# Small matmuls of a chunked scan: heads placed on partitions by the parity of their pair, not of their chunk

## The chip, the core and the metric

The kernel runs on one core of a Trainium2 chip. TensorE (PE in the profile) multiplies through an array of 128 rows by 128 columns; VectorE (DVE), ScalarE (ACT) and GpSimd (POOL) do the elementwise work; SyncE (SP) issues the DMAs here. The metric is device time in microseconds (us), the median of several executions. A row of the profile such as "32*32 32x64" says which part of the array a matmul uses (32 rows, 32 columns) and what it writes (32 partitions by 64 elements).

## What is computed

The reference is one block with an RWKV-7 branch, a short convolution, a cross attention and an MLP, followed by a second block with windowed attention and spatial gating. The change touches the RWKV-7 branch alone. With 8 heads of 64 channels and 512 positions, each head carries a 64x64 state S through the positions:

```
for t in positions:
    S = S * decay[t] + v[t] k[t]^T + (S a[t]) b[t]^T
    y[t] = S r[t]
y = group_norm(y) * ln_x_w + ln_x_b + bonus
out = (y * g) @ w_proj_a
```

The kernel does this in 8 chunks of 64 positions. Within a chunk the recurrence is a triangular system; its two 32x32 diagonal blocks are inverted ahead of time, and the chunk itself is matmuls.

## The kernel before

Everything is one function, `fused_kernel`, written as dataflow on tiles; a scheduler turns it into one fixed order for each engine, higher in the program meaning earlier where operands and buffers allow it. Large projections are done as three matmuls of 128x512 for each weight tile (L182 to L184, weights split in a high and a low part by L152 on ACT and L153 on DVE), and the scheduler fills PE with those of later stages while the scan waits for something.

The eight heads are four pairs j = 0 to 3. `KB` and `AR` hold keys and receptances with the two heads of a pair on partitions 0 to 63 and 64 to 127; `VU` holds, for each chunk and head, 64 rows of v and 64 rows of u (the solution of the triangular system), together 128 partitions. In the kernel before, the chunk's parity c = n % 2 says which half is which: in an even chunk all heads have v on partitions 0 to 63 and u on 64 to 127, in an odd chunk the reverse. The output of a matmul stands on the partitions that answer to the array's columns, so all small matmuls of one chunk use the same half of the columns.

`scan_front(tb)` makes the products of keys and receptances for two chunks (`gram`, L386, masked by L390 on DVE) and inverts the diagonal blocks (`inverse`): the blocks go through DRAM by DMA (L400, L407), 31 steps on DVE (L413, L415) follow, and the inverse comes back by DMA as `ZT` (L419, L425). The loop calls `scan_front(tb + 1)` before the two chunks of tb. `chunk(n, ...)` then is, with its lines:

- L437, L439: the pair's keys are transposed (PE) and copied (ACT) to `KBt`.
- L443: 8 matmuls, one for each head, K = 128 rows, 64 columns, 64 elements each, into the bank `pg`; L447: 4 matmuls of 128 elements add the state's part to it.
- L455, L458, L460: the first 32 rows are copied (ACT), multiplied by the inverse block in 8 matmuls of 32 rows by 32 columns, and copied to `VU` (DVE).
- L462, L464, L467, L469: the second 32 rows: 8 matmuls of 32 by 32 for the correction, copy, 8 matmuls with the inverse block, copy.
- L474, L478, L481: the new state: 4 matmuls of 128x128 with one product for a whole pair, scaled by the decay `PC` (which holds zeros where the heads of a pair must not mix) and added to the old state that POOL has scaled (`spc`, L451). L481 ends the chain that the next chunk's L447 waits for.
- L488, L491: the outputs, 4 matmuls of 128 elements and 8 of 64, into one bank `py` for two chunks. `post(tb)` normalises them.

All of these are plain fp32 matmuls: PE runs each as two passes, each with its own weight load, and the profile counts passes. Eight matmuls stand in a row as x16. Transposes are one pass.

## Time and profile before

| | |
|---|---|
| median of 3 executions | 1340.09 us (1336.71 to 1343.22) |
| the profiled execution: its time, its span | 1343.95 us, 1342.1 us |
| PE busy | 1302.3 us, 97% of the span |
| DVE, ACT, POOL busy | 814.8 us, 520.5 us, 174.4 us |
| DMA queue q1, share of 16 engines | 34.0% |
| granted clock of TensorE, mean | 0.989 |

PE is busy nearly everywhere, but the profile counts a pipelined matmul as busy from its start to its modelled end, so that the time of one row is read from start to start. The granted clock is 1.00 where TensorE runs at 2.4 GHz and 0.5 at 1.2 GHz. The scan's chunks stand in four stretches: the first products at 142 to 152 us, then chunk pairs at 204 to 235, 272 to 305 and 342 to 395 us (two pairs). Between them PE works on large projections while DVE does the 31 steps of the next inverse.

### The profile page before, as it was taken

What the parts mean: (1) busy time and instruction counts of PE and PEld (TensorE: products, weight loads), DVE (VectorE), ACT (ScalarE), POOL (GpSimd) and SP (SyncE); (2) the same over time, 40 slices, a digit from 0 to 9 for tenths busy, and PEclk for the clock granted to TensorE, in tenths of its full rate; (3) what the DMA queues carried; (4) which work ended last, traced back from release to release, by engine and by line L of the source; (5) the groups of instructions that cost most, each with busy time, mean ns of one, the idle gap of its engine ahead of it and who ended that gap; (6) DMA issues with size and microseconds to landing.
All of it is one profiled execution on the core that took longest, in us unless ns stands there. A gap on an engine that the chain in (4) does not pass through costs nothing.

```text
span 1342.1 us, 18317 instructions
## 1 busy us (share of the span) xinstructions
PE 1302.3 (97%) x6626; PEld 1069.7 (80%) x6626; DVE 814.8 (61%) x1631; ACT 520.5 (39%) x940; POOL 174.4 (13%) x184
## 2 busy tenths in 40 slices
PE   3999999999999999999999999999999999999997
PEld 2777888888879888888888888888878777788886
DVE  5677484848466755566854645535676656663455
ACT  4444232322335443454532423323344465333342
POOL 5113002010120010002012020020232000100003
PEclk9999999989999999999999999999999999999999
DMA  4222331314314532143643634332234223233331
GB/s 143 87 79 67 101 104 43 110 44 123 90 63 150 173 110 94 64 149 94 186 152 110 194 112 145 128 96 87 94 126 142 79 63 125 87 97 101 94 118 63
DMA packets 85210, 143.95 MB, mean 107 GB/s; under 512 B 21472, under 2 KB 21600, under 8 KB 85120
## 3 DMA queue, kind: packets, MB, share of 16 engines
q1 hardware_dynamic: 85120, 142.78, 34.0%
q8 instruction: 52, 0.85, 0.3%
q14 instruction: 38, 0.31, 0.1%
HBM read 136.19 MB, written 5.24 MB: 105 GB/s over the span
## 4 chain that ended last, share of the span: by engine, by line
PE 94%; DVE 3%; POOL 1%; DMA 1%; issue 0%; ACT 0%; SPq 0%; DVEq 0%; ACTq 0%; POOLq 0%
PE mm L182 26%; PE mm L183 26%; PE mm L184 25%; PE mm L627 1%; PE mm L628 1%; PE mm L629 1%; PE sc L386 1%; PE ch L943 1%; PE ch L978 1%; PE ch L458 1%; PE ch L467 1%; DMA x<-in_xT 1%; PE sc L974 1%; PE ch L462 1%; PE ch L491 1%; PE ch L474 1%
## 5 line engine op out<-in xcount | busy, mean ns | idle before, releaser
L152 ACT CAST whi<-wraw 128x512 fp32r<-128x512 f32 x406 | 251.7, 621 | 551.7 <-PE mm L183 475.7
L153 DVE TENSOR_TENSOR wlo<-wraw,whi 128x512 fp32r<-128x512 f32 x406 | 298.4, 736 | 228.1 <-PE mm L184 118.6
L182 PE MATMUL mm<-h,whi 128*128 128x512 f32 x328 | 132.5, 404 | 1.0 <-DVE k L237 1.0
L183 PE MATMUL mm<-h,whi 128*128 128x512 f32 x328 | 131.4, 401 | 0.0
L184 PE MATMUL mm<-h,wlo 128*128 128x512 f32 x328 | 131.1, 400 | 0.0
L182 PE MATMUL mm<-x2g,whi 128*128 128x512 f32 x256 | 100.2, 391 | 0.0
L184 PE MATMUL mm<-x2g,wlo 128*128 128x512 f32 x256 | 99.7, 389 | 0.0
L183 PE MATMUL mm<-x2g,whi 128*128 128x512 f32 x256 | 99.6, 389 | 0.0
L182 PE MATMUL mm<-ff,whi 128*128 128x512 f32 x256 | 99.6, 389 | 0.0
L183 PE MATMUL mm<-ff,whi 128*128 128x512 f32 x256 | 99.6, 389 | 0.0
L184 PE MATMUL mm<-ff,wlo 128*128 128x512 f32 x256 | 99.6, 389 | 0.0
L182 PEld LDWEIGHTS mm<-h,whi 128*128 128x128 f32 x328 | 62.8, 192 | 16.2 <-DVE k L237 2.6
L183 PEld LDWEIGHTS mm<-h,whi 128*128 128x128 f32 x328 | 62.7, 191 | 13.1 <-issue 0.4
L184 PEld LDWEIGHTS mm<-h,wlo 128*128 128x128 f32 x328 | 62.5, 190 | 13.3 <-issue 0.5
L852 POOL TENSOR_TENSOR X<-X,d 128x512 f32<-128x512 f32 x24 | 39.3, 1637 | 220.8 <-DVE d L850 220.8
L658 POOL TENSOR_TENSOR gt<-gt,nsq 128x512 f32<-128x512 f32 x21 | 27.7, 1320 | 291.5 <-ACT nsq L657 284.0
L183 PE MATMUL mm<-h2a,whi 128*128 128x512 f32 x152 | 59.7, 393 | 0.4 <-DVE h2a L875 0.4
L184 PE MATMUL mm<-h2a,wlo 128*128 128x512 f32 x152 | 59.8, 393 | 0.0
L182 PE MATMUL mm<-h2a,whi 128*128 128x512 f32 x152 | 59.7, 395 | 0.0
L182 PE MATMUL mm<-h2b,whi 128*128 128x512 f32 x152 | 59.7, 392 | 0.0
L184 PE MATMUL mm<-h2b,wlo 128*128 128x512 f32 x152 | 59.5, 393 | 0.0
L183 PE MATMUL mm<-h2b,whi 128*128 128x512 f32 x152 | 59.5, 392 | 0.0
(465 smaller groups left out, 2700.7 us busy)
## 6 DMA issues: line engine op xcount, KB each, us to landing
wraw<-in_w_in SPq DMA_DIRECT2D x162, 256.0 KB, 2.6
wraw<-in_w_up SPq DMA_DIRECT2D x64, 256.0 KB, 2.6
wraw<-in_w_down SPq DMA_DIRECT2D x64, 256.0 KB, 2.8
adaraw<-in_w_ada SPq DMA_DIRECT2D x24, 512.0 KB, 3.7
wraw<-in_w_proj_b SPq DMA_DIRECT2D x16, 256.0 KB, 2.7
wraw<-in_w_k SPq DMA_DIRECT2D x16, 256.0 KB, 2.6
wraw<-in_w_proj_a SPq DMA_DIRECT2D x16, 256.0 KB, 2.7
wraw<-in_w_v SPq DMA_DIRECT2D x16, 256.0 KB, 2.7
```

Of the source, the lines that this page charges most:

```text
L152: S.copy(hi, src)
L153: eng.tensor_tensor(lo, src, hi.bitcast(F32), op=ALU.subtract)
L182: PE.matmul(acc, lhsT=wh, rhs=xh, start=start and k == 0, stop=False)
L183: PE.matmul(acc, lhsT=wh, rhs=xl, start=False, stop=False)
L184: PE.matmul(acc, lhsT=wl, rhs=xh, start=False, stop=stop and k == n - 1)
L386: PE.matmul(pq[hd % 2][:, j * 128:(j + 1) * 128], lhsT=KB[p0:p0 + 64, j, n * 128:(n + 1) * 128], rhs=AR[p0:p0 + 64, j, n].rearrange("p q c ...
L458: PE.matmul(pu[ub:ub + 32, hs], lhsT=ZT[ub:ub + 32, c, hd, :], rhs=gsb[ub:ub + 32, hs], start=True, stop=True)
L462: PE.matmul(pg[ub + 32:ub + 64, hd * 64:(hd + 1) * 64], lhsT=gr[ub:ub + 32, hd, 32:64], rhs=VU[ub:ub + 32, tb, c, hd, :], start=False, sto ...
L467: PE.matmul(pu[ub + 32:ub + 64, hs], lhsT=ZT[ub + 32:ub + 64, c, hd, :], rhs=gsb[ub + 32:ub + 64, hs], start=True, stop=True)
L474: PE.matmul(pst[:, j * 128:(j + 1) * 128], lhsT=KBt[:, 2 * j:2 * j + 2, :].rearrange("p h f -> p (h f)"), rhs=VU[:, tb, c, 2 * j:2 * j + 2 ...
L658: G.tensor_tensor(self.acc, self.acc, sq, op=ALU.add)
L852: G.tensor_tensor(X[:, j], X[:, j], d, op=ALU.add)
```

## The change

The parity of the pair, j % 2, takes the place of the chunk's parity: pairs 0 and 2 have v on partitions 0 to 63 and u on 64 to 127, in every chunk, pairs 1 and 3 the reverse. The loops over heads run in the order `order8`, in which the pair's parity `jp` changes fastest, so that one matmul writes to the upper half of the partitions and the next to the lower. What follows from it:

- All banks of a chunk hold 256 elements on 128 partitions in place of 512 on 64: `pg`, `pu`, `py`. The copies change with them (one of 128x256 for `gh`; the two halves of `VU` by DVE and ACT, 32x256 each; `y` by one copy for each chunk, from its own bank).
- The 32-row matmuls of the two parities use different rows and different columns of the array, and write the same bank.
- The state's product (L474) becomes 8 matmuls of 64 columns and 64 elements, alternating halves too. The state update is one DVE operation of 256 columns (`s1`) and two of 64x256, and POOL scales `s1` for the chunk after.
- `KB`, `bon`, `g` and the weights `w_lora_g`, `ln_x` are laid out to match: `g` by four activations of 64x256 in place of one of 128x512, for each of four blocks; `KB` by one DVE operation less; `bon` by one more.
- The DMAs of the inverse (to `md` and back to `ZT`) are 8 in place of 4, of half the heads each.
- `gram` puts pairs in another column order, its matmuls are the same.

```
...
-        kb = KB[:, j].rearrange("p (m x) -> p m x", x=256)
-        V.scalar_tensor_tensor(kb[:, :, 64:192], halves(ta), 1.0, halves(m1), op0=ALU.add, op1=ALU.mult)
-        V.tensor_tensor(kb[:, :, 0:64], halves(f)[:, :, 0:64], halves(ip)[:, :, 0:64], op=ALU.mult)
-        V.tensor_tensor(kb[:, :, 192:256], halves(f)[:, :, 64:128], halves(ip)[:, :, 64:128], op=ALU.mult)
+        kb = KB[:, j].rearrange("p (n x) -> p n x", x=128)
+        ub, vb = 64 * (1 - j % 2), 64 * (j % 2)
+        V.scalar_tensor_tensor(kb[:, :, ub:ub + 64], chunks(ta), 1.0, chunks(m1), op0=ALU.add, op1=ALU.mult)
+        V.tensor_tensor(kb[:, :, vb:vb + 64], chunks(f), chunks(ip), op=ALU.mult)
...
-        S.activation(g, p, AF.Copy, scale=0.5)
+        for c in range(2):
+            for jp in range(2):
+                S.activation(g[64 * jp:64 * jp + 64, 256 * c:256 * c + 256],
+                             p[64 * c:64 * c + 64, 256 * jp:256 * jp + 256], AF.Copy, scale=0.5)
...
+    order8 = [(hp, jh, jp) for hp in range(2) for jh in range(2) for jp in range(2)]
...
+        blocks = [(i, d, jp, ((i * 2 + d) * 2 + jp) * 4, 64 * (1 - jp) + 32 * d)
+                  for i in range(2) for d in range(2) for jp in range(2)]
+        for i, d, jp, q0, r0 in blocks:
+            nc.sync.dma_start(md[q0:q0 + 4].rearrange("h j i -> j h i"),
+                              grams[i][r0:r0 + 32, 4 * jp:4 * jp + 4, 32 * d:32 * d + 32])
...
-        for hd in range(8):
-            PE.matmul(pg[ub:ub + 64, hd * 64:(hd + 1) * 64], lhsT=gr[:, hd, 0:64],
-                      rhs=VU[:, tb, c, hd, :], start=hd == 0, stop=n == 0 and hd == 7)
+        for hp, jh, jp in order8:
+            ub, b = 64 * (1 - jp), 2 * jh + hp
+            PE.matmul(pg[ub:ub + 64, b * 64:(b + 1) * 64], lhsT=gr[:, 4 * jp + b, 0:64],
+                      rhs=VU[:, n, 4 * jp + b, :], start=b == 0, stop=n == 0 and b == 3)
...
+        for d in range(2):
+            S.copy(gh[:, d], pg[:, 0:256])
+            for hp, jh, jp in order8:
+                r0, b = 64 * (1 - jp) + 32 * d, 2 * jh + hp
+                hs = slice(b * 64, (b + 1) * 64)
+                PE.matmul(pu[r0:r0 + 32, hs], lhsT=ZT[r0:r0 + 32, c, b, :], rhs=gh[r0:r0 + 32, d, hs],
+                          start=True, stop=True)
+            for jp in range(2):
+                r0 = 64 * (1 - jp) + 32 * d
+                (V.tensor_copy, S.copy)[jp](VU[r0:r0 + 32, n, 4 * jp:4 * jp + 4, :],
+                                            pu[r0:r0 + 32, 0:256].rearrange("p (h v) -> p h v", v=64))
...
-                PE.matmul(pst[:, j * 128:(j + 1) * 128], lhsT=KBt[:, 2 * j:2 * j + 2, :].rearrange("p h f -> p (h f)"),
-                          rhs=VU[:, tb, c, 2 * j:2 * j + 2, :].rearrange("p h v -> p (h v)"),
-                          start=j == 0, stop=j == 3)
+                g0 = 4 * (j % 2) + 2 * (j // 2)
+                for hp in range(2):
+                    PE.matmul(pst[64 * hp:64 * hp + 64, j * 64:(j + 1) * 64], lhsT=KBt[:, 2 * j + hp, :],
+                              rhs=VU[:, n, g0 + hp, :], start=j == 0, stop=j == 3)
...
+                V.tensor_tensor(s1, ps_, comp[0], op=ALU.add)
...
+            for hp in range(2):
+                rows = slice(64 * hp, 64 * hp + 64)
+                V.tensor_tensor(sn[rows, :, 64 * hp:64 * hp + 64], s1[rows], pc[rows], op=ALU.mult)
...
```

The scheduler puts the scan's groups among the large products in another order; behind the scan, PE's order is the same as before. Two places show what moved. The first is PE in chunk 1, between the two products with the inverse block. Rows name line, operation, output and inputs; `gsb` and `gh` are the copies of `pg`, sc the banks of `gram`. Before:

```order
L458 MATMUL ch_1586<-gsb_1585,ZT_1351 32x64 x8
L386 MATMUL sc_1682<-AR,KB 128x128
L386 MATMUL sc_1681<-AR,KB 128x128
L386 MATMUL sc_1682<-AR,KB 128x128
L386 MATMUL sc_1681<-AR,KB 128x128
L462 MATMUL ch_1570<-VU,gram_1224 32x64 x8
L386 MATMUL sc_1682<-AR,KB 128x128
L183 MATMUL mm_2894<-h_2_112,whi_2897 128x512
L184 MATMUL mm_2894<-h_2_112,wlo_2898 128x512
L182 MATMUL mm_2894<-h_2_112,whi_2897 128x512
L467 MATMUL ch_1586<-gsb_1585,ZT_1351 32x64 x8
```

and with the change:

```order
L461 MATMUL ch_1615<-gh_1616,ZT_1371 32x64 x8
L392 MATMUL sc_1733<-AR,KB 128x128 x2
L392 MATMUL sc_1732<-AR,KB 128x128
L470 MATMUL ch_1614<-VU,gram_1240 32x64
L392 MATMUL sc_1733<-AR,KB 128x128
L392 MATMUL sc_1732<-AR,KB 128x128
L470 MATMUL ch_1614<-VU,gram_1240 32x64 x7
L392 MATMUL sc_1733<-AR,KB 128x128
L183 MATMUL mm_3002<-h_3_113,whi_3011 128x512
L184 MATMUL mm_3002<-h_3_113,wlo_3012 128x512
L461 MATMUL ch_1615<-gh_1616,ZT_1371 32x64 x8
```

The correction (L462, now L470) is cut in one and seven, and the two banks of `gram`, which belong to the two row halves of the array, no longer alternate strictly.

The second place is PE between the state's product of chunk 1 and the first use of that state in chunk 2. Before:

```order
L474 MATMUL ch_1615<-VU,KBt_1568 128x128 x4
L491 MATMUL ch_1554<-VU,gram_1224 64x64 x8
L443 MATMUL ch_1819<-VU,gram_1356 64x64 x8
L184 MATMUL mm_2894<-h_3_113,wlo_2904 128x512
L182 MATMUL mm_2894<-h_3_113,whi_2903 128x512
L183 MATMUL mm_2894<-h_3_113,whi_2903 128x512
L184 MATMUL mm_2894<-h_3_113,wlo_2904 128x512
L182 MATMUL mm_2894<-h_3_113,whi_2903 128x512
L183 MATMUL mm_2894<-h_3_113,whi_2903 128x512
L437 MATMUL sc_1812<-ident,KB 128x128 x4
L447 MATMUL ch_1819<-state_1620,AR 64x128 x4
```

and with the change:

```order
L478 MATMUL ch_1659<-VU,KBt_1612 64x64 x2
L498 MATMUL ch_1674<-state_1223,AR 64x128
L478 MATMUL ch_1659<-VU,KBt_1612 64x64 x6
L498 MATMUL ch_1674<-state_1223,AR 64x128 x3
L502 MATMUL ch_1674<-VU,gram_1240 64x64 x8
L449 MATMUL ch_1879<-VU,gram_1380 64x64 x8
L454 MATMUL ch_1879<-state_1224,AR 64x128 x4
```

The large products and the transposes that stood ahead of the state's first use now stand behind it.

## Rows read from the trace of the kernel before

**Rows 1.** The page, the chain that ended last, shares of the span by engine.

```profile
PE 94%; DVE 3%; POOL 1%; DMA 1%; issue 0%; ACT 0%; SPq 0%; DVEq 0%; ACTq 0%; POOLq 0%
```

**Rows 2.** Busy us (and count) by engine, clock, DMA share, three stretches.

```profile
204.00:235.00 31.00, 30.74 (x281) 25.57 (x280) 14.24 (x23) 6.55 (x11) 6.81 (x10) 0.94 0.15 40
272.00:305.00 33.00, 32.87 (x282) 27.59 (x282) 13.66 (x23) 6.62 (x12) 6.34 (x9) 0.84 0.21 57
342.00:395.00 53.00, 51.74 (x480) 41.99 (x479) 27.61 (x55) 15.86 (x29) 10.86 (x9) 1.00 0.26 78
```

**Rows 3.** PE groups by line and form: passes, busy us, mean ns, idle before.

```profile
L458 PE MATMUL ch<-gsb,ZT 32*32 32x64 f32 x128 | 8.6, 216 | 0.0
...
L443 PE MATMUL ch<-VU,gram 128*64 128x64 f32 x128 | 8.8, 222 | 0.0
...
L474 PE MATMUL ch<-VU,KBt 128*128 128x128 f32 x56 | 9.1, 316 | 0.0
...
L447 PE MATMUL ch<-state,AR 128*64 128x128 f32 x56 | 7.5, 276 | 1.3 <-DVE state L481 1.3
```

**Rows 4.** PE in order of time in chunks 0 and 1: start, length, passes.

```profile
204.46 0.71 PE L386 MATMUL sc<-AR,KB 64*128 64x128 f32 x4
205.10 1.08 PE L458 MATMUL ch<-gsb,ZT 32*32 32x64 f32 x16
206.11 0.72 PE L386 MATMUL sc<-AR,KB 64*128 64x128 f32 x8
...
216.47 0.71 PE L447 MATMUL ch<-state,AR 128*64 128x128 f32 x5
...
217.08 0.27 PE L488 MATMUL ch<-state,AR 128*64 128x128 f32 x1
217.13 0.27 PE L447 MATMUL ch<-state,AR 128*64 128x128 f32 x1
217.19 0.27 PE L488 MATMUL ch<-state,AR 128*64 128x128 f32 x1
```

**Rows 5.** PE in the windowed attention, outputs of 512 in one bank.

```profile
1067.85 1.08 PE L978 MATMUL ch<-apT,vtok 128*64 128x512 f32 x4
...
1089.24 1.61 PE L978 MATMUL ch<-apT,vtok 128*64 128x512 f32 x4
```

**Rows 6.** The chain that ended last, 213 to 226 us: start, its share of time.

```profile
213.25 1.38 PE ch L474 x8
...
222.82 1.01 PE ch L467 x16
223.83 0.43 PE mm L183
224.25 0.23 PE mm L184
...
224.95 0.89 PE ch L474 x8
```

**Rows 7.** DVE and ACT groups of 512 and of 256 columns: busy, mean ns.

```profile
L460 DVE COPY VU<-ch 32x512 f32<-32x512 f32 x8 | 5.5, 684 | 19.1 <-PE ch L458 19.1
...
L153 DVE TENSOR_TENSOR pT<-sc,pT 128x256 fp32r<-128x256 f32 x16 | 6.7, 422 | 4.4 <-ACT pT L152 4.3
...
L152 ACT CAST pT<-sc 128x256 fp32r<-128x256 f32 x16 | 6.0, 373 | 7.5 <-DVE pT L153 3.9 <-PE sc L717 3.7
...
L373 ACT ACTIVATE gt<-mm 128x512 f32<-128x512 f32 x4 | 2.4, 596 | 6.3 <-PE mm L371 6.3
```

**Rows 8.** Waits of PE over the span: total us, times, longest.

```profile
PE ch L447 <- DVE state L481: 1.3, 1, 1.3
```

**Rows 9.** SP and PE in order of time: the second inverse's return, its first use.

```profile
203.63 1.80 SPq L425 DMA_DIRECT2D ZT<-zd  x4
...
272.74 1.08 PE L458 MATMUL ch<-gsb,ZT 32*32 32x64 f32 x16
```

More of the change, by code (lines that the diff above doesn't have):

```diff
@@ L419, in inverse, with chunk @@
             nc.sync.dma_start(zv[k], Z[32 * k:32 * k + 32])
-        ZT = tt("ZT", (128, 2, 8, 32))
-        for i in range(2):
-            ub = 64 * (1 - i)
-            for d in range(2):
-                q0 = (i * 2 + d) * 8
-                nc.sync.dma_start(ZT[ub + 32 * d:ub + 32 * d + 32, i], zd[q0:q0 + 8].rearrange("h c i -> c h i"))
-        return ZT
-    state = [None]
-    ybank = [None]
-    def chunk(n, gr, ZT):
-        tb, c = n // 2, n % 2
-        kb, ub = 64 * c, 64 * (1 - c)
-        sp = state[0]
+        ZT = tt("ZT", (128, 2, 4, 32))
+        for i, d, jp, q0, r0 in blocks:
+            nc.sync.dma_start(ZT[r0:r0 + 32, i], zd[q0:q0 + 4].rearrange("h c i -> c h i"))
+        return ZT
+    states = [tmp("state", (128, 4, 128), bufs=2) for _ in range(2)]
+    for st in states:
+        G.memset(st, 0.0)
+    comp = [None]
+    def chunk(n, gr, ZT, y):
+        c = n % 2
+        sp, sn = states[(n + 1) % 2], states[n % 2]
         pt = scbank()
@@ L454, in chunk @@
-        pu = chbank()
-        S.copy(gsb[ub:ub + 32], pg[ub:ub + 32])
-        for hd in range(8):
-            hs = slice(hd * 64, (hd + 1) * 64)
-            PE.matmul(pu[ub:ub + 32, hs], lhsT=ZT[ub:ub + 32, c, hd, :], rhs=gsb[ub:ub + 32, hs],
-                      start=True, stop=True)
-        V.tensor_copy(VU[ub:ub + 32, tb, c], pu[ub:ub + 32].rearrange("p (h v) -> p h v", v=64))
-        for hd in range(8):
-            PE.matmul(pg[ub + 32:ub + 64, hd * 64:(hd + 1) * 64], lhsT=gr[ub:ub + 32, hd, 32:64],
-                      rhs=VU[ub:ub + 32, tb, c, hd, :], start=False, stop=hd == 7, skip_group_check=True)
@@ L464, in chunk @@
-        S.copy(gsb[ub + 32:ub + 64], pg[ub + 32:ub + 64])
-        for hd in range(8):
-            hs = slice(hd * 64, (hd + 1) * 64)
-            PE.matmul(pu[ub + 32:ub + 64, hs], lhsT=ZT[ub + 32:ub + 64, c, hd, :], rhs=gsb[ub + 32:ub + 64, hs],
-                      start=True, stop=True)
-        V.tensor_copy(VU[ub + 32:ub + 64, tb, c], pu[ub + 32:ub + 64].rearrange("p (h v) -> p h v", v=64))
+                ub, jh = 64 * (1 - j % 2), j // 2
+                PE.matmul(pg[ub:ub + 64, jh * 128:(jh + 1) * 128], lhsT=AR[:, j, n, 0, :],
+                          rhs=sp[:, j, :], start=False, stop=jh == 1)
@@ new lines, in chunk @@
+        for d in range(2):
[5 more added lines that the diff above has]
+                          start=True, stop=True)
+            for jp in range(2):
+                r0 = 64 * (1 - jp) + 32 * d
+                (V.tensor_copy, S.copy)[jp](VU[r0:r0 + 32, n, 4 * jp:4 * jp + 4, :],
+                                            pu[r0:r0 + 32, 0:256].rearrange("p (h v) -> p h v", v=64))
+            if d == 0:
+                for hp, jh, jp in order8:
+                    ub, b = 64 * (1 - jp), 2 * jh + hp
+                    PE.matmul(pg[ub + 32:ub + 64, b * 64:(b + 1) * 64], lhsT=gr[ub:ub + 32, 4 * jp + b, 32:64],
+                              rhs=VU[ub:ub + 32, n, 4 * jp + b, :], start=False, stop=b == 3, skip_group_check=True)
@@ L486, in chunk @@
+        py = chbank()
         if n > 0:
             for j in range(4):
-                PE.matmul(py[kb:kb + 64, j * 128:(j + 1) * 128], lhsT=AR[:, j, n, 1, :],
-                          rhs=sp[:, j, :], start=j == 0, stop=False)
-        for hd in range(8):
-            PE.matmul(py[kb:kb + 64, hd * 64:(hd + 1) * 64], lhsT=gr[:, hd, 64:128], rhs=VU[:, tb, c, hd, :],
-                      start=n == 0 and hd == 0, stop=hd == 7)
+                vb, jh = 64 * (j % 2), j // 2
+                PE.matmul(py[vb:vb + 64, jh * 128:(jh + 1) * 128], lhsT=AR[:, j, n, 1, :],
+                          rhs=sp[:, j, :], start=jh == 0, stop=False)
@@ L494, in heads, with post @@
+        for hp, jh, jp in order8:
+            vb, b = 64 * jp, 2 * jh + hp
+            PE.matmul(py[vb:vb + 64, b * 64:(b + 1) * 64], lhsT=gr[:, 4 * jp + b, 64:128], rhs=VU[:, n, 4 * jp + b, :],
+                      start=n == 0 and b == 0, stop=b == 3)
+        S.copy(y[:, 256 * c:256 * c + 256], py[:, 0:256])
     def heads(ap):
         return ap.rearrange("p (h v) -> p h v", v=64)
-    def post(tb):
-        y = tt("y")
-        S.copy(y, ybank[0])
+    def post(tb, y):
         bv = tt("bv")
-        for c in range(2):
-            rows = slice(64 * c, 64 * c + 64)
-            G.tensor_tensor(heads(bv[rows]), VU[rows, tb, c], bon[rows, tb, :].unsqueeze(2).to_broadcast([64, 8, 64]),
-                            op=ALU.mult)
+        bvv = bv.rearrange("p (c b v) -> p c b v", c=2, v=64)
+        ns = slice(2 * tb, 2 * tb + 2)
+        for jp in range(2):
+            rows = slice(64 * jp, 64 * jp + 64)
+            G.tensor_tensor(bvv[rows], VU[rows, ns, 4 * jp:4 * jp + 4, :],
+                            bon[rows, ns, :].unsqueeze(3).to_broadcast([64, 2, 4, 64]), op=ALU.mult)
@@ L609, in fused_kernel @@
             ts_ = slice(tb * 128, (tb + 1) * 128)
-            split(p.rearrange("p (j t) -> p j t", t=128), ya[:, :, 0, ts_], ya[:, :, 1, ts_])
+            yav = [ya[:, :, i, ts_].rearrange("p j (c t) -> p j c t", c=2) for i in range(2)]
+            split(p.rearrange("p (c j t) -> p j c t", c=2, t=64), yav[0], yav[1])
     merged = [regionr("merged0"), regionr("merged1")]
```

75 lines of the change are left out of this document (36 added, 39 removed).

## The prediction

> **What bounds the kernel now.** I read the chain that ended last first: 94% of it is PE [rows 1], so time comes off this kernel mainly where PE has less to do or waits less. Then the three stretches with chunk pairs, by window: PE is busy for 30.74 of 31, 32.87 of 33 and 51.74 of 53 us [rows 2], because large products fill every wait; DVE and ACT are busy for half of that time or less. So inside the scan, too, an us saved on PE is an us of the total, as long as the filling holds. The groups by form say how many passes there are [rows 3], and the timeline what one takes from start to start, which is not its length: the lengths overlap.
>
> Three spacings matter. Sixteen passes of 64 elements on one place of the array take 1.08 us, the last one 0.216 long: (1.08 - 0.216) / 15 = 0.058 us each [rows 3, 4]. Five passes of 128 elements on one column half take (0.71 - 0.276) / 4 = 0.109 each [rows 3, 4]. Where L447 and L488, which write different halves, stand in alternation, the starts are 0.05 to 0.06 apart, so that each half still goes at 0.11 and both run at once [rows 4]. The attention shows the same within one bank: four passes of 512 on two halves end after 1.08 us where they fall together and after 1.61 where they do so only in part [rows 5]. Two row halves overlap as well: 8 passes of L386 in 0.72 us, against 4 in 0.71 with one half [rows 4]. The change asks for this overlap everywhere in the chunk.
>
> **What the change takes away.**
> - Passes of 64 elements: L458, L462 and L467 (32 by 32) and L443 and L491 (64 columns) have 128 passes each, 640 in all; one group of each form is in [rows 3]. They stay as many. With two halves at once, 0.029 in place of 0.058 each: 640 x 0.0288 = 18.4 us. No row shows this at 64 elements, only at 128 and 512; the bounds are nothing and 18.4, and I take the upper one, since at 128 elements the halving is complete [rows 4].
> - Passes of 128 elements: L447 and L488, 56 each. Alone they would take 112 x 0.109 = 12.2 us; in four of the chunks a stretch as in [rows 4] overlaps already, about 0.28 each, so 11.1. Alternating, 112 x 0.055 = 6.2: 4.9 us less, both ends known from rows.
> - The state's product, L474: 56 passes at 0.89 / 8 = 0.11 [rows 6], 6.2 us. It becomes 112 passes of 64 elements and 64 columns: 3.2 us at 0.029, 6.5 at 0.058. I take 3.0 less.
>
> Together 26.3 us.
>
> **What it adds.**
> - Changes of the array's shape. By PE's order, the stretch up to the end of the scan has 93 changes between full, 64-row, 64-column and 32 by 32 use, and 113 with the change: the cut of L470 in one and seven puts other work between. A trip out and back costs about 0.3: L467's 16 passes take 1.01 where 16 x 0.058 = 0.92, and the large product behind it 0.43 where the next one takes 0.23 [rows 6]. At 0.16 for each change, 20 cost 3.2 us.
> - `gram`: in the new order some 15 of its matmuls run without a partner of the other row half, 30 passes at 0.11 in place of 0.055 [rows 4]: 1.7 us.
> - The state's way. Three DVE operations of 256 columns at 0.42 [rows 7] and about 0.3 of hand-over lie between L478 and L454, 1.6 us. In four places PE has only three matmuls of L498, L502 and L449 for that time, 6 x 0.055 + 32 x 0.029 = 1.26 us, with the next large product queued behind the waiting L454. So 4 x 0.35 = 1.4 us. Before, large products stood there and PE waited once, for 1.3 [rows 8].
> - Four activations in place of one for each block of `g`: ACT has 4 x 0.37 = 1.5 in place of 0.6 us [rows 7], just ahead of the first weight casts of the next stage. PE has gram's matmuls at that point, which cover it; uncovered it would be about 1 us, once. I take nothing.
> - Eight DMAs in place of four on SP, each way: 1.8 us more, since four take 1.80 [rows 9]. The way back has time: issued at 203.63, first used at 272.74 [rows 9]. Weight loads queue behind it on SP and are fetched several tiles ahead, which hides it; if that cover were gone, it would cost at most 4 x 3.6 us. The shorter copies (`gh`, `VU`: 0.37 and 0.42 in place of 0.58 to 0.68 [rows 7], the former taken from casts and sums of that size) and the one operation less for `KB` stand beside PE work and give nothing.
>
> **The clock.** In the first two stretches the granted clock is 0.94 and 0.84, in the third, where large products stand between all groups, 1.00 [rows 2]. So part of the time runs at 1.2 GHz, which stretches L474 from 0.89 to 1.38 [rows 6]. What that took is 0.06 x 31 + 0.16 x 33 = 7.1 us. The clock fell after groups of small matmuls mixed with L386. With the change these groups are shorter, but the mixture with gram (L392) is still there. The bounds are all of it back and none; on the far side, a third stretch at 0.84 as well would cost 8.5. I take half of 7.1 back, 3.5.
>
> **The sum.** -18.4 - 4.9 - 3.0 + 3.2 + 1.7 + 1.4 - 3.5 = -23.5 us. From the profiled execution's 1343.95 that is 1320.4; it lies 3.9 above the median, so the median goes from 1340.1 to about 1317.
>
> **The rivals.**
> - A floor for each pass. In the trace of before no sustained run of passes starts less than about 0.055 apart, whether 64 elements on one place, 128 on two halves, or two row halves [rows 4]. Streaming explains all three, but so would a floor for issuing a pass with its weight load. Then 64 elements gain nothing: the 640 passes stay at 0.058, L474 costs 0.3 more, L447 and L488 still give 4.9, and the additions 3.2 + 1.7 with little waiting: -4.9 + 0.3 + 4.9 + 0.4 = +0.7, 1341. For it: the coincidence. Against it: starts 0.05 apart at 128 are just what the halves' streaming gives, with nothing on top. A floor between gives a part: at 0.040, some 11 of the 18.4.
>  The Trainium skill speaks for this one: TensorEngine Tiling (Array Packing), Instruction Overhead, gives every matmul an overhead of about 60 cycles and advises against taking the tiling factor from a dimension that is already small, as 64 elements are. No row here separates the two.
> - One bank. The 32 by 32 matmuls of the two parities use different row groups and write one bank, `pu` or `pg`. L978 shares a bank between column halves, but with all rows [rows 5], and L386's row halves have a bank each, so no row shows this. If such pairs take turns, 384 passes lose 0.0288 each, 11.1 us, and half of the clock's gain goes: -10.6, 1329.5.
>  That pair is what the Trainium skill warns of: TensorEngine Tiling (Array Packing), Restrictions and Gotchas, says that different row tiles cannot use the same PSUM bank at the same time. It is written of row tiles, and nothing before shows whether it holds where the partitions differ.
> - Slower: a change of place costs like a change of shape. If stepping from one 32 by 32 place to the other empties the array as stepping to another shape does, 0.09 each [rows 6], then three groups of eight in eight chunks make 192 steps, 17.3 us, the 11.1 of these passes is lost and the clock gives nothing: -23.5 + 11.1 + 17.3 + 3.5 = +8.4, 1348. Slower begins at 0.046 a step. Against it: stepping between column halves costs nothing that shows [rows 4].
>
> **How the numbers follow.** Forecast 0.58 (1317; by itself 1309 to 1326, from the clock's bounds and a few us of waits), the floor 0.22, the bank 0.10, slower steps 0.06, and 0.04 for stalls of the fixed order that no row tells of. A measurement of this kernel tells about 0.5% from no change, 6.7 us. Faster by more: forecast, bank and half of the rest, 0.70. Within: the floor and a little, 0.23. Slower: 0.07. To hold 8 in 10 the range must take in the floor: 1308 to 1341.
>
> **What would show it.** In the profile after: groups of x16 of L449, L461, L470, L478 and L502 at about 0.65 us in place of 1.08, with starts some 0.03 apart. All at 1.08: the floor. L461 and L470 at 1.08 and L449 at 0.65: the bank. L461 above 1.5: the steps. L454 waiting for `state` in the four places, 0.3 to 0.4 each; large products after a change at 0.43; the granted clock of the two stretches above 0.9. The prediction is wrong if PE shows gaps in the scan beyond 3 us, if the clock falls in the third stretch, or if the groups shrink and the end doesn't follow.

## The result, and the profile after

The changed kernel takes 1331.25 us (1330.82 to 1333.88, 7 executions) against 1340.19 (1336.71 to 1343.22, 7 executions): a ratio of 0.9936, interval 0.992 to 0.9951. It is 8.9 us faster where 23 were forecast. The time lies in the range, 1308 to 1341, but not in the forecast's own, 1309 to 1326. The profiled execution took 1332.02, with a span of 1330.3; against the profiled execution before that is 11.9 less, with a mean clock of 0.989 in both.

What was to get shorter got shorter. In order of time on PE (start, length, line, passes), the last part of chunk 0 and the start of chunk 1 (L449) in the kernel after:

```profile
208.51 0.64 PE L461 MATMUL ch<-gh,ZT 32*32 32x64 f32 x16
...
209.97 0.34 PE L478 MATMUL ch<-VU,KBt 128*64 128x64 f32 x4
210.14 0.28 PE L502 MATMUL ch<-VU,gram 128*64 128x64 f32 x2
...
210.77 0.57 PE L478 MATMUL ch<-VU,KBt 128*64 128x64 f32 x12
211.17 0.58 PE L502 MATMUL ch<-VU,gram 128*64 128x64 f32 x13
211.53 0.27 PE L449 MATMUL ch<-VU,gram 128*64 128x64 f32 x1
211.59 0.22 PE L502 MATMUL ch<-VU,gram 128*64 128x64 f32 x1
211.64 0.63 PE L449 MATMUL ch<-VU,gram 128*64 128x64 f32 x15
```

Sixteen passes of 32 by 32 take 0.64 us where they took 1.08 [rows 4]: (0.64 - 0.215) / 15 = 0.028 a pass, half of 0.058. The 64-column groups go at nearly the same rate. The step out of a group stays as long as it was: 0.14 from the start of its last pass to the start of the matmul behind it, before [rows 4] and after (the large product behind this L461 starts at 209.08).

But some groups no longer stand in one piece, and large products stand between the pieces:

```profile
206.18 0.29 PE L470 MATMUL ch<-VU,gram 32*32 32x64 f32 x2
206.40 0.50 PE L184 MATMUL mm<-h,wlo 128*128 128x512 f32 x1
206.73 0.40 PE L182 MATMUL mm<-h,whi 128*128 128x512 f32 x1
207.06 0.63 PE L470 MATMUL ch<-VU,gram 32*32 32x64 f32 x14
```

Between L470's first matmul and the other seven, which wait for ACT's half of `VU`, PE goes to the full shape and back. The pieces take 0.22 and 0.56 from start to start, together what the uncut group would take plus 0.21.

PE's waits from the first chunk on have grown from the one of 1.3 us [rows 8] (total us, times, longest; the row left out lies ahead of the chunks). Those for the state are five of 0.2 to 0.5 us and one of 2.1:

```profile
PE ch L454 <- DVE state L489: 4.2, 6, 2.1
...
PE sc L392 <- DVE gram L396: 1.1, 1, 1.1
PE mm L183 <- DVE ob L153: 1.1, 1, 1.1
PE mm L182 <- ACT ob L152: 0.6, 1, 0.6
PE ch L470 <- DVE VU L465: 0.4, 1, 0.4
```

The windows of the three stretches with chunk pairs (busy us and count of PE, PEld, DVE, ACT, POOL; then granted clock, DMA share, GB/s), wider than in [rows 2] because the chunks now lie earlier. First the kernel before in the same windows:

```profile
200.00:235.00 35.00, 34.74 (x299) 28.86 (x298) 15.27 (x25) 8.89 (x15) 6.81 (x10) 0.95 0.19 50
260.00:305.00 45.00, 44.87 (x335) 37.35 (x334) 24.01 (x52) 11.36 (x20) 7.49 (x11) 0.89 0.22 60
325.00:395.00 70.00, 68.74 (x555) 56.06 (x554) 41.41 (x102) 21.68 (x38) 11.91 (x10) 1.00 0.27 81
```

and the changed kernel:

```profile
200.00:235.00 35.00, 34.51 (x340) 26.74 (x339) 21.44 (x47) 11.27 (x23) 9.85 (x12) 1.00 0.31 80
260.00:305.00 45.00, 42.38 (x379) 33.45 (x378) 29.81 (x72) 13.11 (x27) 8.91 (x11) 1.00 0.34 87
325.00:395.00 70.00, 66.77 (x583) 48.48 (x582) 36.45 (x82) 24.76 (x51) 12.55 (x10) 0.88 0.24 76
```

The clock has changed places. The first two stretches, at 0.95 and 0.89 before, are at 1.00; the third, at 1.00 before, is at 0.88: TensorE ran there at 1.2 GHz for 17 us in a row, from 361 to 378. How much of this is the kernel's and how much this execution's had to be found out.

Where the time went can be summed on PE from each start to the next one. The part taken goes from the 381st to the 1161st large product (512 elements), which holds all chunks; "large, beyond 0.227" is what the 780 large products took above 0.2267 us each: the steps between them and other shapes, the waits behind them, and their share of the lower clock. The columns on the right are runs told below; s_after is the changed kernel again, measured later. In us:

| | before | after | s_after | e1 | e6 |
|---|---|---|---|---|---|
| 32 by 32 groups | 25.1 | 16.8 | 15.4 | 22.3 | 13.6 |
| 64-column groups, the state's product, transposes | 44.8 | 30.8 | 30.9 | 35.6 | 29.4 |
| gram | 13.7 | 14.6 | 14.6 | 14.4 | 14.3 |
| large, beyond 0.227 each | 15.2 | 24.4 | 20.3 | 17.0 | 15.3 |
| the whole part | 275.7 | 263.4 | 258.1 | 266.1 | 249.4 |
| of it at 1.2 GHz | 20.5 | 20.5 | 10 | 14 | 0 |

The small groups gave some 22 us of the 26.3 forecast, and the large products took 5 to 9 back. Of the time at 1.2 GHz, 3 to 7 us lie ahead of the first chunk, near 132 us, in all of these traces but e6's.

### The profile page after: what moved, and what is told of

Read it like the earlier page. It is cut to its first block, busy times and chain, and to the rows that moved or that the text cites. A ratio compares the mean times of both kernels' runs of the same rounds, so it can differ in the third digit from the quotient of the medians.

```text
span 1330.3 us, 18533 instructions
## 1 busy us (share of the span) xinstructions
PE 1283.8 (97%) x6682; PEld 1045.2 (79%) x6682; DVE 815.2 (61%) x1639; ACT 526.6 (40%) x972; POOL 175.6 (13%) x186
## 4 chain that ended last, share of the span: by engine, by line
PE 92%; DVE 4%; ACT 1%; issue 1%; DMA 1%; POOL 0%; SPq 0%; DVEq 0%; ACTq 0%; POOLq 0%
PE mm L183 26%; PE mm L182 25%; PE mm L184 25%; PE mm L643 1%; PE mm L642 1%; PE mm L641 1%; PE sc L392 1%; DMA wraw<-in_w_in 1%; PE ch L957 1%; PE ch L461 1%; PE ch L992 1%; PE sc L988 1%; PE ch L470 1%; DVE state L489 1%; DVE wlo L153 1%
## 5 line engine op out<-in xcount | busy, mean ns | idle before, releaser
L153 DVE TENSOR_TENSOR wlo<-wraw,whi 128x512 fp32r<-128x512 f32 x406 | 298.6, 737 | 234.1 <-PE mm L184 125.1
L672 POOL TENSOR_TENSOR gt<-gt,nsq 128x512 f32<-128x512 f32 x21 | 27.7, 1319 | 296.4 <-ACT nsq L671 289.0
```

The costliest lines, as they stand in the source:

```text
L153: eng.tensor_tensor(lo, src, hi.bitcast(F32), op=ALU.subtract)
L672: G.tensor_tensor(self.acc, self.acc, sq, op=ALU.add)
```

## The experiments

Behind the result there were four things to tell apart: what the alternation itself is worth, what cutting L470 costs, why the state is late, and what the clock has to do with it. Since the clock differs between executions of one kernel, the granted clock is given beside a time where it matters, and the changed kernel and the three most important variants were run a second time, side by side.

**e1: the new placing without the alternation.** Each group does one half first, then the other; L454, L478 and L498 likewise.

```
-    order8 = [(hp, jh, jp) for hp in range(2) for jh in range(2) for jp in range(2)]
+    order8 = [(hp, jh, jp) for jp in range(2) for hp in range(2) for jh in range(2)]
...
-            for j in range(4):
+            for j in (0, 2, 1, 3):
```

> The changed kernel with the same placing of the heads, but every group of small matmuls does one column half first and then the other (L449, L454, L461, L470, L478, L498, L502). Theory 1, that the gain is the overlap of two halves: 16 passes of 64 elements go back from 0.45 to 0.57 us to about 1.0, L454 and L498 from 0.055 to 0.11 a pass, in all some 20 us more than the changed kernel, 1351, and so about 10 slower than the kernel before. Rival, that it came from the new layout (copies of 256 columns, the state's product without the zero blocks): little changes, 1331 to 1336. On the clock: if TensorE falls to 1.2 GHz in the third stretch of chunks because the halves alternate, that fall (17 us long, worth about 7.5) is gone and the time is about 1343; if the order of the work and its waits let it fall, it stays.

1336.04 us (1333.79 to 1341.3, 12 executions), ratio 0.9968 (0.995 to 0.9986). The time is 15 us under the first theory's and at the edge of the rival's, whose reason fails, since the groups did get slower. First, the alternation was not gone. PE in order of time:

```profile
206.67 0.88 PE L461 MATMUL ch<-gh,ZT 32*32 32x64 f32 x16
...
208.77 0.63 PE L478 MATMUL ch<-VU,KBt 128*64 128x64 f32 x11
209.18 0.27 PE L502 MATMUL ch<-VU,gram 128*64 128x64 f32 x1
209.24 0.22 PE L478 MATMUL ch<-VU,KBt 128*64 128x64 f32 x1
209.29 0.22 PE L502 MATMUL ch<-VU,gram 128*64 128x64 f32 x1
209.29 0.22 PE L478 MATMUL ch<-VU,KBt 128*64 128x64 f32 x1
```

A group of 32 by 32 takes 0.88 us, between 0.64 and 1.08. And L502's passes start among L478's, although in PE's instruction order all of these L478 stand first:

```
707 L478 MATMUL ch_1582<-VU,KBt_1539 64x64 x7
708 L502 MATMUL ch_1597<-VU,gram_1227 64x64 x6
```

PE thus starts a matmul of the other column half ahead of older ones that wait for their own half; of L461's second half the first pass starts when three of the first half's eight have still to start (the "five passes" in the expectation of e7 is a miscount). L470 alone stands in two pieces of four matmuls here, with large products between them, so that its halves do not overlap at all. Second, the 10.3 us that the small groups lost (5.5 and 4.8 in the table) came to only 4.8 at the end: the large products' excess fell from 24.4 to 17.0, since L454 waited for 0.4 us in all in place of 4.2, and less of the part ran at 1.2 GHz. A part of this is the clock of the executions: read at the same clock, as is done below, the two kernels are 6.8 apart. So about a third of what even this partial alternation gives in the changed kernel is lost again. The third stretch is at 1.00 in this trace, but the repeats below show that one trace decides nothing there.

**e2: L470 in one piece.** ACT's half of `VU` lands later than DVE's; the group now begins with it.

```
-                for hp, jh, jp in order8:
+                for hp, jh, jq in order8:
+                    jp = 1 - jq
                     ub, b = 64 * (1 - jp), 2 * jh + hp
                     PE.matmul(pg[ub + 32:ub + 64, b * 64:(b + 1) * 64], lhsT=gr[ub:ub + 32, 4 * jp + b, 32:64],
```

> The changed kernel with L470's matmuls in the order in which the later of the two VU copies (ACT's) comes first, so that the eight stand together and no large products are put between them. Theory: each of the eight cuts costs a trip to the large shape and back, 0.21 us on the large products and some 0.15 on the small group, 8 x 0.36 = 3 us, so about 1328 with the clock as it is. Rival: the large products have to be done somewhere, their trip is only moved and the group waits longer for its copy: within 1 us of 1331.

1322.53 (1322.05 to 1324.38, 5 executions), ratio 0.9862 (0.9837 to 0.9888): 8.7 us less than the changed kernel had taken, where 3 were expected. In the trace the trip costs what was expected: the group takes 0.57 from start to start in place of 0.22 + 0.56, and one visit of large products with its 0.21 is gone, 8 x 0.42 = 3.4 us if all eight cuts are like this one. Summed over all of them, on the part of the table and with time at 1.2 GHz counted half (an estimate), the small groups give 1.7 back and the large products 0.3 to 0.9, so it is nearer 2 to 2.5: some of the large products' trips are only moved, as the rival had it. Much of the rest was clock: 0.994 in the mean here, 0.988 in the seven executions of the changed kernel. The runs side by side, below, say what remains of it.

**e7: how far PE reaches ahead.** The half changes after every two matmuls (on top of e2).

```
-    order8 = [(hp, jh, jp) for hp in range(2) for jh in range(2) for jp in range(2)]
+    order8 = [(hp, jh, jp) for hp in range(2) for jp in range(2) for jh in range(2)]
```

> The kernel with L470 in one piece, with the column half changing after every two matmuls instead of every one (L449, L461, L470, L502). With halves of four matmuls a group of 32 by 32 took 0.81 us, with halves of one 0.57, and in the former the second half's passes began five passes ahead of the first half's end. If PE starts passes that far ahead whenever the other half is free, two matmuls (four passes) at a time overlap fully: 0.57 to 0.6 us, 1322 to 1324. If overlap needs neighbours in different halves: 0.7 or more, some 4 us over the kernel with L470 in one piece, 1327.

1323.65 (1321.94 to 1325.13, 4 executions), ratio 0.9871 (0.9851 to 0.9892), against e2's 1322.53.

```profile
207.86 0.66 PE L461 MATMUL ch<-gh,ZT 32*32 32x64 f32 x16
```

0.66 against 0.64: neighbours need not differ in their half, as long as the other half's work is within a few passes. (A second trace of this kernel, below, gives 1324.39.)

**e3 and e4: the rest of the chunk pair later.** `post(tb)` is written behind the first chunk of the next pair; e4 is e3 and e2 in one.

```
         for c in range(2):
             chunk(2 * tb + c, grams[tb][c], zts[tb], y)
+            if c == 0 and tb > 0:
+                post(tb - 1, yl)
+        yl = y
...
-        post(tb, y)
```

> The changed kernel with post(tb) written behind the first chunk of the next pair, so that POOL's L515 and L517 and DVE's L519 to L530 no longer stand ahead of that chunk's state. Theory: in the third stretch DVE operations were stretched from 0.16 or 0.69 to 1.2 to 1.5 us while POOL worked, and the state came 2.1 us late; L454 then waits under 1 us in that stretch, where it waited 2.8, so -2 us. If that wait of PE is what lets the clock fall behind it, the fall (17 us long, worth 7.5) goes too: about 1321. Rival: the clock falls with the mixture of small groups and large products, whatever the wait: 1329. If post is now in the way of something else (the last y, the first chunk of the next pair): 1333 or more.

> Both edits of the two runs before in one kernel. If they are independent and the clock's fall hangs on the wait: 1331 - 3 - 2 - 7.5 = 1318. If the clock falls all the same: 1326.

e3: 1329.16 (1328.34 to 1330.89, 6 executions), ratio 0.9911 (0.9888 to 0.9935). The third stretch is at full clock, but the first and the second are at 0.90 and 0.89, and PE's waits in the scan are no fewer:

```profile
PE ch L454 <- DVE state L489: 3.6, 4, 1.4
PE ch L470 <- DVE VU L465: 2.5, 2, 1.4
```

The time is that of the rival, but the clock fell in other stretches than the one it spoke of. So the edit only moved the trouble, and decides nothing. e4: 1321.88 (1320.18 to 1327.38, 6 executions), ratio 0.9858 (0.9832 to 0.9884): between its two expectations, and not to be told from e2 alone.

**e5: without POOL's last bonus.** The clean test of the late state: the instruction order of all engines is that of the changed kernel, less three POOL operations (L515 twice, L517).

```
-        for jp in range(2):
+        for jp in range(2 if tb < 3 else 0):
...
-        G.tensor_tensor(bv, bv, lnb, op=ALU.add)
+        if tb < 3:
+            G.tensor_tensor(bv, bv, lnb, op=ALU.add)
+        else:
+            bv = lnb
```

> The changed kernel without POOL's last L515 and L517, the bonus of the last two chunks, whose product is replaced by ln_x_b alone (so this part of the computation is left out); the order of every other instruction on every engine is the same. In the changed kernel these three POOL operations ran from 354.1 to 358.3 us, DVE operations beside them took 1.2 to 1.5 us in place of 0.16 to 0.69, PE waited 2.1 us for the state, and TensorE's clock fell for 17 us right behind that wait. Theory: POOL's work slowed DVE and the wait let the clock fall, so the wait goes down to under 0.5, the fall in this stretch is gone, and the time is 2 + 7 less: about 1322. Rival 1, the clock falls with the mixture of groups there and not with the wait: 1329. Rival 2, DVE was late for another reason: wait and time stay, 1331.

1322.35 (1319.72 to 1322.81, 4 executions), ratio 0.9858 (0.9837 to 0.9879), the time that the first theory gave. DVE in the changed kernel, in order of time (what it waited for stands in brackets):

```profile
353.54 0.43 DVE L465 COPY VU<-ch 32x256 f32<-32x256 f32 x1 [0.82 <-PE ch L461]
...
354.36 1.33 DVE L153 TENSOR_TENSOR wlo<-wraw,whi 128x512 fp32r<-128x512 f32 x1 [0.20 <-PE mm L184]
355.61 1.53 DVE L529 TENSOR_TENSOR y<-y,bv 128x512 f32<-128x512 f32 x1
357.06 1.24 DVE L138 SCALAR_TENSOR_TENSOR rq_t<-rq_t,rq_v 128x2 f32<-128x2 f32 x1
358.33 0.43 DVE L484 TENSOR_TENSOR s<-ch,cn 128x256 f32<-128x256 f32 x1
```

POOL at the same time:

```profile
352.86 1.28 POOL L528 TENSOR_TENSOR y<-y,lnx 128x512 f32<-128x512 f32 x1 [3.82 <-DVE y L527]
354.10 2.50 POOL L515 TENSOR_TENSOR bv<-VU,bon 64x512 f32<-64x512 f32 x2
356.67 1.61 POOL L517 TENSOR_TENSOR bv<-bv,lnx 128x512 f32<-128x512 f32 x1
```

and PE:

```profile
355.18 0.57 PE L478 MATMUL ch<-VU,KBt 128*64 128x64 f32 x12
...
357.63 0.40 PE L183 MATMUL mm<-h,whi 128*128 128x512 f32 x1
360.17 0.66 PE L454 MATMUL ch<-state,AR 128*64 128x128 f32 x8 [2.14 <-DVE state L489]
```

The same operations of DVE in e5, where POOL has nothing to do from 352.3 on:

```profile
352.52 0.69 DVE L153 TENSOR_TENSOR wlo<-wraw,whi 128x512 fp32r<-128x512 f32 x1 [0.20 <-PE mm L184]
353.13 0.68 DVE L532 TENSOR_TENSOR y<-y,bv 128x512 f32<-128x512 f32 x1
353.73 0.15 DVE L138 SCALAR_TENSOR_TENSOR rq_t<-rq_t,rq_v 128x2 f32<-128x2 f32 x1
353.96 0.42 DVE L484 TENSOR_TENSOR s<-ch,cn 128x256 f32<-128x256 f32 x1
```

and of PE in e5:

```profile
355.80 0.39 PE L183 MATMUL mm<-h,whi 128*128 128x512 f32 x1
356.12 0.66 PE L454 MATMUL ch<-state,AR 128*64 128x128 f32 x8
```

PE's waits for the state in e5, all of them:

```profile
PE ch L454 <- DVE state L489: 2.1, 5, 0.5
```

With POOL at work, an operation on two columns took 1.24 us in place of 0.15 and ended with POOL's; without it, the state came in time and PE did not wait there. The state's own operations were not slower (L484 took 0.43 and 0.42). What was late is their start: L478 ends at 355.75, but DVE reaches L484 at 358.33 only, since L153, L529 and L138 stand ahead of it and take 4.1 us in all in place of 1.5. That POOL made the state late is shown, and rival 2 falls. The clock stayed at 1.00 in this stretch, so the theory's second half looked proven as well; the repeats below take it back.

**e6: the bonus early, all of the computation.** The bonus needs only v, which is there before the scan. On top of e2 it is written ahead of the two chunks.

```
-    def post(tb, y):
-        bv = tt("bv")
+    def bonus(tb):
+        bv = tt("bv")
...
+        return bv
+
+    def post(tb, y, bv):
...
+        bv = bonus(tb)
         y = tt("y")
```

> The kernel with L470 in one piece (1322.5), and with the bonus written ahead of the two chunks instead of behind them: it needs only v, so POOL can do it while DVE works on the inverse. All of the computation is there. Theory: L454's waits in the third stretch (2.3 of 4.4 us) and the fall of the clock behind them (7 us long, 2.5 lost) go: about 1318. Rival: the contention of POOL with DVE moves to the steps of the inverse, which are then late, and the chunks wait for ZT: 1323 or more.

1318.87 (1317.62 to 1321.19, 5 executions), ratio 0.9841 (0.9821 to 0.9861): 21 us under the kernel before, and the best of all kernels here. All three stretches are at 1.00, the small groups are whole, and L454's waits are down from 4.2 to

```profile
PE ch L454 <- DVE state L490: 2.1, 5, 0.5
```

**e8: e6 without the alternation,** with the edit of e1.

> The kernel with L470 in one piece and the bonus early (1318.9), with every group doing one column half first and then the other, as in e1. In its trace a group of 32 by 32 should take 0.81 us in place of 0.57 and the 64-column groups some 4.8 us more in all. Theory: what alternation gives in PE time, 24 x 0.24 + 4.8 = 10.6 us, reaches the end only where waits and the clock don't take it back; in e1 against the changed kernel only 5 of it did. With the late state and the falls of the clock gone, nearly all should: 1318.9 + 10.6 less the 2.1 of L454's waits that a longer PE covers = 1327 to 1329.5. Rival: alternation is worth no more than e1 showed, and the rest is covered in any case: 1324.

1330.39 (1329.03 to 1332.38, 6 executions), ratio 0.9931 (0.9909 to 0.9953): 11.5 slower than e6, a little more than expected (10.6 less 2.1). PE no longer waits for the state at all in this trace, so the 2.1 are covered as expected; but the clock, 1.00 in e6's second stretch, is down (0.992 in the mean, 0.995 in e6), which is worth 3 to 4 us and leaves about 8 for the alternation:

```profile
260.00:305.00 45.00, 43.10 (x348) 34.75 (x347) 24.63 (x57) 11.79 (x24) 5.77 (x9) 0.85 0.29 74
```

**e9: the bonus early in the kernel before,** with the same edit and nothing else.

> The kernel before, with the bonus written ahead of the two chunks, as in e6, and nothing else. Theory: in the kernel before the groups are long enough to cover the state, PE waits for it once, 1.3 us, so that is all there is to gain: 1339 to 1341. Rival: moving POOL's work is worth in any kernel what it was worth in e5 and e6: 1332 to 1336.

1343.27 (1341.52 to 1357.68, 12 executions), ratio 1.0041 (1.0014 to 1.0068): no gain, if anything a small loss, most of it clock (0.988 in the mean, 0.992 in the kernel before beside it); its wait for the state is 1.0 in place of 1.3. What e5 and e6 gain was thus not to be had before. It belongs to the shorter groups, which leave DVE and POOL less PE work to hide behind.

**The changed kernel, e7 and e5 once more,** one execution each, on one chip.

> The changed kernel once more, unchanged, for a second trace. In three traces with a wait of 2.1 to 2.3 us ahead of L454 in the third stretch (the changed kernel, e2, e7) the clock fell behind it for 17, 7 and 0 us; in no trace without that wait did it fall in that stretch. Theory: the wait lets the clock fall, more or less long, so here it falls again behind L454, near 361 us. Rival: the fall in the first trace was this one execution's, and the second has none there though it has the wait.

> The kernel of e7 once more, unchanged, for a second trace: it has the wait of 2.2 us and had no fall behind it. Theory: whether the fall comes differs from one execution to the next, so this one may have it, 3 to 17 us long. Rival: this kernel's rows ahead of the wait keep the clock up each time, and there is none again.

> The kernel of e5 once more (without the bonus of the last two chunks on POOL), for a second trace: no wait of 2 us, so by the theory no fall in the third stretch in this execution either. Rival: falls there come and go without the wait, and this trace has one.

1324.6, 1324.39 and 1321.45. The changed kernel has its wait of 2.1 us again, and behind it, unlike the first time, no fall; e7, which had none behind its wait of 2.2, has one of 7 us now. The third stretch of the changed kernel:

```profile
325.00:395.00 70.00, 66.75 (x649) 51.62 (x646) 42.00 (x91) 29.94 (x60) 12.55 (x10) 1.00 0.30 91
```

and of e7, this time:

```profile
325.00:395.00 70.00, 66.90 (x629) 52.26 (x625) 41.25 (x90) 29.22 (x59) 12.75 (x10) 0.95 0.29 87
```

So the same rows of PE come with and without the fall. e5 has none in this stretch again, but one in the second. The theory's expectation for r_after is wrong, its rival's right; for r_e7 it is the other way round: a wait of 2 us makes a fall possible at most, and 1331 is not this kernel's fixed time.

**The changed kernel, e5, e2 and e6 side by side,** five rounds on one chip.

> The changed kernel again, side by side with e5, e2 and e6 on one chip, 5 rounds. Theory A, the lower clock (0.988 over 7 executions) belongs to the kernel, through the wait of 2.1 us in the third stretch: again about 0.988 to 0.990 in the mean, about 1330. Theory B, it was those executions' or that chip's, as the second trace suggests (0.994, 1324.6, no fall behind the same wait): the mean clock is like that of the other three here, 0.993 to 0.995, and the time is 1324 to 1326.

> The kernel of e5 again (without the bonus of the last two chunks on POOL). Both theories: about 1322. Theory A: 8 us less than the changed kernel beside it, with a mean clock 0.005 or more higher. Theory B: only the wait's 2 to 3 us less, at the same clock.

> The kernel of e2 again (L470 in one piece). By its trace the cut costs 3.4 us. Theory A: 8 less than the changed kernel beside it, 5 of them by the clock. Theory B: 3 to 4 less, at the same clock.

> The kernel of e6 again (L470 in one piece, the bonus early). Theory A: 12 less than the changed kernel beside it. Theory B: 3.4 for the cut and 2 to 3 for the wait, 6 less, at about the same clock; 1319 in either case.

| | time | executions | ratio to before (interval) | mean clock |
|---|---|---|---|---|
| s_after | 1327.85 (1325.24 to 1332.43) | 6 | 0.9907 (0.9883 to 0.9932) | 0.991 |
| s_e5 | 1322.66 (1321.73 to 1323.32) | 4 | 0.9862 (0.9840 to 0.9884) | 0.994 |
| s_e2 | 1324.04 (1322.57 to 1324.49) | 4 | 0.9871 (0.9848 to 0.9893) | 0.993 |
| s_e6 | 1319.90 (1318.08 to 1321.98) | 4 | 0.9842 (0.9818 to 0.9866) | 0.995 |

Neither theory holds whole. Of the differences to the changed kernel, e5's 5.2 and e6's 8.0 lie between B (2 to 3, 6) and A (8, 12), and e2's 3.8 is B's. Its clock is lower than theirs here too, by 0.002 to 0.004, but it is not 0.988. Over all executions (14 of the changed kernel, 55 of the kernel before, 9 each of the three) the mean clocks are 0.990, 0.991, and 0.994 to 0.995, and each kernel's times lie on a line against the clock, 1.2 us for 0.001 in the kernel before (1335.51 at 0.994 to 1347.72 at 0.985), 1.1 in the changed one and 0.4 to 0.8 in the other three. Read from these lines at 0.9945, where all of them have executions or nearly, the kernel before stands at 1336.9, the changed one at 1324.6, e2 at 1322.7, e5 at 1322.1 and e6 at 1319.7. So at the same clock the change gives 12 us; the whole group another 2, POOL's absence 2.5, both edits of e6 5; and on top of that the mean clock is worth another 4 to 5 to these three over the changed kernel.

That last gain can't be put down to the edits. The mean takes in falls of the clock outside the scan: near 53 and 132 us, ahead of the first chunk, and near 1036 us, behind the scan. They come and go from trace to trace, 0 to 14 us in all. The stretch ahead of the first chunk in e2:

```profile
130.00:145.00 15.00, 13.07 (x104) 10.64 (x104) 6.35 (x12) 8.46 (x20) 2.28 (x5) 1.00 0.26 75
```

and in s_e2:

```profile
130.00:145.00 15.00, 12.89 (x62) 10.45 (x63) 5.98 (x9) 8.62 (x21) 3.36 (x7) 0.77 0.21 60
```

s_e2 has a lower mean, 0.993 against 0.995, though its scan ran at full clock throughout and e2's did not. Within the scan, 195 to 400 us, TensorE ran at 1.2 GHz for 14 us in the trace of the kernel before, for 17, 3 and 3 in the three of the changed kernel, and for 0 to 7 in the seven of e2, e5 and e6.

## Why the prediction was right and wrong

Three terms of the sum failed. The passes of 64 elements gave some 14.5 us where 18.4 were forecast, PE's waits grew by 5 to 6 where 1.4 was forecast, and the clock took 3 us in the executions of the result where it was to give 3.5. All three signs that the prediction named for being wrong came: gaps of PE in the scan beyond 3 us, a fall of the clock in the third stretch, and an end that followed the groups only in part.

**The overlap: right in mechanism, and in size within a group.** 0.64 us for 16 passes where about 0.65 was forecast. The floor for each pass falls: a whole group goes at 0.028 a pass, half of the supposed floor. The slower steps fall with it. The bank falls too: L461's two halves use different rows and write one bank, `pu`, and overlap fully. Its time, 1329.5, is nevertheless within 2 us of the result; a time that fits does not show a mechanism. The Trainium skill's rule that different row tiles cannot use the same PSUM bank at the same time (TensorEngine Tiling (Array Packing), Restrictions and Gotchas) thus does not hold here, where the tiles differ in columns and partitions too. The overhead of about 60 cycles for each matmul that the same page of the Trainium skill gives (Instruction Overhead) would be 0.025 us at 2.4 GHz, an estimate from the page's figure; passes 0.028 apart leave room for it, so no run here tests it. What falls is a floor of 0.055. Over all 640 passes the gain is smaller than 18.4 all the same, 14.5: 1.7 of the difference is L470's cut, which e2 gives back. A part of the rest is probably the step out of each group, 0.14 as before, which the forecast halved with the passes.

**L447, L488 and L474: about right.** L454 does 8 passes of 128 elements in 0.66 us, on one half they would take 7 x 0.109 + 0.28 = 1.04; the state's product takes 0.17 + 0.40 of PE's time in chunk 0 (from start to start, 209.97 to 210.14 and 210.77 to 211.17 in the first rows above) where L474 took 0.89 [rows 6]. One reason given was wrong: L447 and L488 overlapped before [rows 4] not because the order alternated them, but because PE reached ahead, as e1 shows.

**Changes of shape: about right.** 3.2 forecast for 20 more; the cut of L470, which makes most of them, costs 2 to 2.5 by the sums under e2, and e2 is 2 faster at the same clock. Without the waits, the large products' excess is 2.6 to 3.2 more than before.

**The state's wait: too small.** Forecast: 1.4, as four waits of 0.35. There were six, 4.2 in all (3.7 and 3.9 in the other two traces), one of them 2.1. Five of them, 2.1 in all, are of the kind that was forecast; the sixth is not. The step that failed is that DVE's way to the state was counted from L478's end, with nothing ahead of it on DVE and without POOL; e5 shows what three operations ahead of it cost beside POOL. The waits for `gram` (1.1, and 0.4 in the other two traces), for two casts (1.1 and 0.6) and of L470 for `VU` (0.4) stood in no term of the sum: PE came there and found them unfinished. Against the 1.3 before, all this is 5 to 6 more, some 4 more than forecast.

**The clock: a gain that can't be relied on.** Forecast: 3.5 back, as half of 7.1. By the means over all executions, 0.991 before and 0.990 after, the change gains nothing there and loses about 1; in the seven executions of the result it was 0.988, 3 us worse than the kernel before. The second stretch did get better: of four traces with long groups (the kernel before, e1, e8, e9) all have falls there, of the twelve with the alternation and `post` in its place four. But the third, which was to stay at 1.00, fell in three of the seven traces with the long wait ahead of L454 (the changed kernel, e2 and e7, each run two or three times), and in none of the eleven without it. In the scan alone, two of the changed kernel's three traces ran 10 us less at 1.2 GHz than the kernel before, which is worth more than the 3.5, and one ran 3.5 us more. e2, e5 and e6 come with a clock of 0.994 to 0.995, but as their falls outside the scan differ too, that fewer waits and whole groups raise it is not shown.

**From the profiled execution to the median: wrong.** The 3.9 us between them were carried over as if they were fixed. They are mostly the clock: the profiled execution before ran at 0.989, the mean is 0.991, and 0.002 is worth 2.4 us by the line above. In the changed kernel's profile the difference was 0.8.

Term by term, the kernel before against the three traces of the changed kernel, on the part of the table above, with waits apart and time at 1.2 GHz counted half (an estimate):

| us | forecast | found |
|---|---|---|
| passes of 64 elements | -18.4 | -14.5 |
| passes of 128 elements | -4.9 | -4.6 |
| the state's product | -3.0 | -2.4 |
| changes of shape (found: on the large products alone) | +3.2 | +2.6 to +3.2 |
| gram | +1.7 | +1.2 |
| waits | +1.4 | +5 to +6 |
| transposes | 0 | -0.3 |
| together | -20.0 | -12.4 |
| the clock, by the means | -3.5 | +3 (the result), +1 (all executions) |

The lines against the clock give the same 12. e6, in which the group is whole and POOL out of the way, takes 1319 to 1320: nearly what was forecast for the change alone, but partly by a higher clock. At the same clock it is 17 under the kernel before, where the forecast had 20.

What stays open: what decides whether the clock falls behind a given row. The same rows of PE came with a fall and without one (the changed kernel and r_after, e7 and r_e7), and three of seven against none of eleven makes the wait a likely cause of the falls in the third stretch, not a proven one. In the second stretch the kernel before has two falls without any wait of PE near them.

## What to carry to other kernels

Small matmuls that use only half of the array's columns, such as these in fp32, can run two at a time without a change to their number or size; give neighbours different halves, and keep a group in one piece. Then look at what the longer PE time had covered: the chain over DVE and what stands ahead of it there, POOL's operations beside it, the next stage's casts. And compare times at the same mean clock: here executions of one kernel differ by more than the cut, the wait and the casts together.

## What was not expected of the hardware

- PE does not keep to its instruction order across column halves: it started the other half's matmuls ahead of about three older passes that were queued for the busy half. With four matmuls on one half and then four on the other a group took 0.88 us, with two and two 0.66, with one and one 0.64, and 1.08 with all eight on one half.
- An operation of DVE on 128x2 elements took 1.24 us beside POOL's 128x512 and ended with it, 0.15 without; operations of 128x512 with two inputs took 1.33 and 1.53 in place of 0.69. The copy L465, with one input, took its usual 0.43 beside POOL's L528. That agrees with the Trainium skill (GPSIMD Engine Reference, Specifications), by which POOL shares its SBUF interfaces with VectorE and contends with operations that have two SBUF inputs.
- TensorE's granted clock differed between executions of the same kernel on the same chip, 0.985 to 0.994 in the kernel before, and the time with it: 12 us from end to end, as much as the change gives at the same clock.
